# Two late norms' sums of squares on VectorE, and other round sizes in the first ConvGLU

## The chip, the cores and the metric

The kernel runs on one core of a Trainium2 chip. The metric is the device time of one execution in microseconds. A core has five engines with a queue of instructions each: TensorE (PE in the profile, its weight loads PEld), VectorE (DVE), ScalarE (ACT), GpSimd (POOL) and SyncE (SP), which here issues the weight transfers. Each engine works through its queue in order; semaphores make it wait for others. SBUF is the working memory; PSUM, which takes TensorE's results, has eight banks of 512 numbers on each of 128 partitions.

## The reference: what is computed

Two layers over 512 latent tokens and 256 context tokens of width 1024. The first mixes tokens by windowed attention, the second by a bidirectional gated linear recurrence (HGRN2). Each layer ends with a ConvGLU of inner width 2816. Before every mixer and every ConvGLU stands an RMS norm with a scale and a shift. Cut to what matters here:

```python
def rms_norm(x, gain):
    y = x * lax.rsqrt(jnp.mean(x * x, axis=-1, keepdims=True) + EPS)
    return y * gain

def conv_glu(h, w_up, conv_w, conv_b, w_down):
    gate, val = jnp.split(h @ w_up, 2, axis=-1)
    return (jax.nn.silu(dwconv3(gate, conv_w, conv_b)) * val) @ w_down

# each layer
hx = rms_norm(x, norm1_g) * (1 + sc1) + sh1      # and hc from ctx
x  = x + g1 * mixer(hx, hc)                      # and ctx in the first layer
hx2 = rms_norm(x, norm2_g) * (1 + sc2) + sh2
x  = x + g2 * conv_glu(hx2, ...)                 # and ctx in the first layer
```

## The kernel before

**Layout.** The streams lie transposed in SBUF: eight tiles d of 128 features by tokens, `xl` for the 512 latent tokens and `xc` for the 256 context tokens. Every product is done in a split form: each operand is a high part (a ScalarE copy) and a low part (a VectorE subtraction of the high part), and a k tile takes three TensorE products, high by high, high by low and low by high. `load_w` makes such weight operands: one transfer into a raw buffer (two of them, tag `wr`), then per operand the copy at L117 and the subtraction at L118. An operand (`operand`, L84) is a pair of 512-column buffers, taken in turn from several pools; in the first ConvGLU these are one of four pairs and one of two.

**Norms.** A norm needs the sum over all features of x squared, for each token. `square_acc` takes a tile d: ScalarE squares it (L513), into the accumulator `acc` itself for the first tile, else into a buffer `sq` of which there are two; then an addition puts it into `acc` (L515). `row_factor` sums `acc` over the partitions with TensorE (`nss`, L524), takes the power -0.5 on GpSimd (L429), builds a diagonal on VectorE (L529) and spreads it with TensorE (`nR`, L533) into the row factor `R`. The factor is multiplied in after the next product, so that product needs only the scaled but not yet normalized operand that `scaled` makes: a ScalarE copy with a scale (L362) and a VectorE instruction for the low part (L363).

`square_acc` is called in three places. In `attn_out`, the norm ahead of the first ConvGLU, the addition is on VectorE. In `done0`, which the last round of the first ConvGLU calls for each finished tile d, and in `hgrn_out`, ahead of the second ConvGLU, it is on GpSimd.

**The first ConvGLU.** `ffn` (L958) works on 22 column tiles of the inner width. `up(ft)` loads the two weight blocks of a tile, computes gate and value, by seven products of half size (`gate_pair`), the convolution, the SiLU and the product, and leaves the split tile `g` in one of five buffers (pool `gpA`, five, L1345). A round holds some column tiles, as `ROUNDS[0]` says: after its tiles it computes one tile of the next round ahead, and then the down product of its own. The down product takes four passes `dp`; a pass loads the weights of 256 output features for all tiles of the round, as two halves (`cols=True`: an operand holds four k tiles of 128 columns, so a half with more than four takes a second operand), and works on two output tiles d of 128 features. Each d takes two PSUM banks (latent and context) of the eight, and six TensorE products per tile of the round, and ends with two VectorE instructions that add the gated result to `xl` and `xc` (L1023). In the last round nothing is computed ahead; there the first pass does all tiles but the last for both halves before the last one:

```python
part = dp == 0 and not ahead
if part:
    for j in range(2):
        down(j, range(nf - 1))
```

and `done0` runs for tile d after the L1023 of tile d+1: squares and sum, then `scaled` for the recurrence's input `hn2`.

**After it.** `hgrn` takes over the PSUM banks for its own pools and begins with `front(0)`: `pf`, whose weights are loaded like the others, over all eight k tiles of `hn2`. Only after that product comes `row_factor`. At its end `hgrn_out` does the output product `ho`, adds it to `xl` (L895), and scales and squares each tile; the second ConvGLU's first gate product `pd` runs before its `row_factor`.

**Order.** The program order isn't the order on the engines. A planner simulates the timeline while the kernel is built, and puts ready instructions on each engine by priority, which is the program order, save that weight splits are moved ahead (`high_priority(offset=W_AHEAD)`, 180 places). The result is a fixed queue for each engine.

Of the kernel before, what the change touches and what calls it, by code (L numbers as in the profile page):

```python
# [12 lines left out]
ALU = mybir.AluOpType  # L13
# [14 lines left out]
NFF = DFF // P  # L28
EPS = 1e-6
NEG = -1e30  # L30
ROUNDS = ((3, 4, 4, 4, 3, 4), (8, 7, 7))
W_AHEAD = 180
PER_UNIT = 3.2

# [38 lines left out]
class Kernel:  # L73
# [430 lines left out]
    def segs(self, lat_only):  # L504
        return [(0, LAT, self.xl)] + ([] if lat_only else [(LAT, TOK, self.xc)])

    def square_acc(self, d, acc, lat_only, tmp, tag="ny", first=None, eng=None):
        nc = self.nc
        n = LAT if lat_only else TOK
        first = d == 0 if first is None else first  # L510
        sq = acc if first else tmp.tile([P, TOK], F32, tag=tag, name="sq", bufs=2)
        for lo, hi, x in self.segs(lat_only):
            nc.scalar.activation(sq[:, lo:hi], x[:, d], AF.Square)  # L513
        if not first:
            (eng or nc.vector).tensor_tensor(acc[:, :n], acc[:, :n], sq[:, :n], op=ALU.add)  # L515

    def row_factor(self, acc, lat_only, tmp, pp, tag, width, R, sh, dg):

# [439 lines left out]
    def ffn(self, l, hs, R, rows, lat_only, tmp, acp, bk, gp, done, side=None):  # L958
# [14 lines left out]
        def up(ft):  # L973

            ws_ = [self.wcols(wup, ft * P, P), self.wcols(wup, DFF + ft * P, P)]
            ops = self.load_w(ws_) if lat_only else self.load_pair(ws_, tmp)
            if side:
                next(side, None)

            G = tmp.tile([P, 2 * half + 2], F32, tag="G", name="G", bufs=gb)  # L980
            gg = tmp.tile([P, 2 * half], F32, tag="ny", name="gg", bufs=2)
            (self.gate_plain if lat_only else self.gate_pair)(ft, ops, hs, G, gg, R, rows, half, tmp, bank)
            nc.vector.tensor_copy(ap(G[:, 0:1], 0, (TW + 1, nv)), G[:, 1 + SH:1 + SH + nv])
            cb = tmp.tile([P, 2], F32, tag="cb", name="cb")
            nc.vector.tensor_scalar(cb[:, :nv], G[:, 1 + SH:1 + SH + nv], ws[:, ft:ft + 1], cw[:, 66 + ft:67 + ft], op0=ALU.mult, op1=ALU.add)
            u = tmp.tile([P, n], F32, tag="nt", name="u", bufs=gb)
            nc.scalar.activation(u, G[:, 1:1 + n], AF.Copy, scale=cw[:, 22 + ft:23 + ft])
            nc.vector.scalar_tensor_tensor(u, G[:, 0:n], cw[:, ft:ft + 1], u, op0=ALU.mult, op1=ALU.add)
            nc.vector.scalar_tensor_tensor(u, G[:, 2:2 + n], cw[:, 44 + ft:45 + ft], u, op0=ALU.mult, op1=ALU.add)
            for v, c, m in segs:  # L990
                nc.scalar.activation(u[:, c:c + m], u[:, c:c + m], AF.Silu, bias=cb[:, v:v + 1])
                nc.vector.scalar_tensor_tensor(gg[:, c:c + m], gg[:, c:c + m], gg[:, SH + v:SH + v + 1], u[:, c:c + m],
                                               op0=ALU.subtract, op1=ALU.mult)
            g2 = gp.tile([P, 2, n], F32R, tag="g", name="g")
            nc.scalar.activation(g2[:, 0], gg[:, :n], AF.Copy)  # L995
            nc.vector.tensor_tensor(g2[:, 1], gg[:, :n], f(g2[:, 0]), op=ALU.subtract)
            return g2

        f0, late, ahead = 0, None, []
        for r, nf in enumerate(ROUNDS[l]):  # L1000
            gt = ahead + [up(ft) for ft in range(f0 + len(ahead), f0 + nf)]
# [272 lines left out]
    def hgrn_out(self, part, hn, acc, tmp, pj):  # L1274
        nc = self.nc
        self.shifts(1, 1, hn)
        wout = self.a["hgrn_w_out"][0]
        oh = part[0]
        act = lambda k: (oh[:, 0, k], oh[:, 1, k])
        for dp in range(KT // 2):  # L1280
            if dp < 2:
                w, ps, ks = part[1][dp], part[2][dp], (KT - 1,)
            else:
                w = self.load_w([self.wcols(wout, d * P, P) for d in (dp, dp + 4)])
                ps = pj.tile([P, 1024], F32, tag="pj", name="ho")
                ks = range(KT)
            for j in range(2):
                d = dp + 4 * j
                pd = ps[:, 512 * j:512 * j + 512]
                for _ in self.mm_steps(w[j], ks, act, [(pd, 0)], first=dp >= 2):  # L1290
                    pass
                self.add_gated(1, 2, d, pd, True)
            for d in (dp, dp + 4):
                self.scaled(1, 1, d, hn, True)
                self.square_acc(d, acc, True, tmp, "sg", first=(d == 0), eng=nc.gpsimd)


    def dump(self, name, t):
# [3 lines left out]
    def run(self, stop=99):  # L1302
        nc, a = self.nc, self.a
# [26 lines left out]
        tmp = self.pool(es, "tmpA", 1)  # L1330
        acp = self.pool(es, "accA", 1)
        acc = Rp.tile([P, TOK], F32, tag="acc", name="acc0")
# [20 lines left out]
        accs = []  # L1353

        def done0(d, bank):
            if d == 0:
                hn2.append(self.hn_tile(hb, "hn2"))
                accs.append(Rp.tile([P, TOK], F32, tag="acc", name="acc1"))
                self.shifts(1, 0, hn2[0])
            self.square_acc(d, accs[0], False, tmp, eng=nc.gpsimd)  # L1360
            self.scaled(1, 0, d, hn2[0], False)

        self.ap_, self.ap_tag = Rp, "acc"
        self.ffn(0, hs, R, rows, False, tmp, acp, bk, gp, done0, (x for r in (0, 1, 2) for x in self.ada_steps(1, r, bk, "ps", 512)))
        if stop == 3:
            self.dump_x(); rs.close(); es.close(); hss.close(); hB.close(); pjs.close(); top.close(); return
# [15 lines left out]
        acc = Rp.tile([P, LAT], F32, tag="acc", name="acc2")  # L1382
# [10 lines left out]
        tmp = self.pool(es, "tmpB", 2)  # L1393
# [59 lines left out]
```

## Time and profile before

| | us |
|---|---|
| median of 3 runs | 1876.24 |
| lowest and highest run | 1875.39, 1877.27 |
| profiled execution | 1872.88 |
| its span in the profile | 1871.1 |
| TensorE busy | 1801.3 (96%) |
| VectorE busy | 1214.1 (65%) |
| GpSimd busy | 247.4 (13%) |
| mean granted TensorE clock | 0.988 |

Times in the profile count from the start of the span. Busy time is the time in which an engine has an instruction in it. A row of a timeline gives the start, the duration, the engine, the line, the operation, the output and inputs by the program's names, the shapes and a count, where neighbouring instructions of a kind are put together; in brackets stands the idle time of the engine before it, and what ended that. The granted clock is the share of its full rate that TensorE was given.

### The profile page before, as it was taken

Reading aid. Unit: us, or ns where it says so; the run is one execution under the profiler, and the core shown is the slowest. Engines: PE = TensorE matmul, PEld = TensorE weight load, DVE = VectorE, ACT = ScalarE, POOL = GpSimd, SP = SyncE. Lnnn points to the kernel's source line nnn. Section 1 sums busy time; section 2 is a strip of 40 time slices with the busy share of each in tenths; the row PEclk is TensorE's granted clock in tenths of the full one; section 3 lists DMA queues with packets and bytes.
Section 4 is the critical chain, followed back from the end, with each engine's and each line's share of the span. In section 5 each row is a group of like instructions: output and inputs, shape, how many; then the busy total and the mean of one; then the engine's idle time right before and its main releaser. Section 6 shows DMA issues by size and latency. Waiting matters only on the chain.

```text
span 1871.1 us, 32302 instructions
## 1 busy us (share of the span) xinstructions
PE 1801.3 (96%) x13326; PEld 1576.9 (84%) x13326; DVE 1214.1 (65%) x2243; ACT 754.7 (40%) x1478; POOL 247.4 (13%) x233
## 2 busy tenths in 40 slices
PE   6999999998999999999998999999998999999998
PEld 4976786787888888989887888988886799899997
DVE  5575667466867686766777676777676655455462
ACT  4354555465534252434354333333332443233332
POOL 1233333103201000101013101111110200000000
PEclk9999999998999999999998999999999999999999
DMA  9204104232333333233313212122220332333321
GB/s 309 66 23 158 47 24 169 68 102 68 124 113 102 113 124 113 91 113 124 113 61 90 58 35 58 35 57 58 57 69 24 90 91 91 90 96 96 92 82 65
DMA packets 204416, 166.44 MB, mean 89 GB/s; under 512 B 5149, under 2 KB 198254, under 8 KB 199150
## 3 DMA queue, kind: packets, MB, share of 16 engines
q1 hardware_dynamic: 196608, 160.47, 27.8%
q10 hardware_dynamic: 7662, 3.92, 0.7%
q8 instruction: 105, 1.72, 0.4%
q14 instruction: 41, 0.34, 0.1%
HBM read 162.27 MB, written 2.10 MB: 88 GB/s over the span
## 4 chain that ended last, share of the span: by engine, by line
PE 87%; DVE 5%; DMA 4%; issue 2%; ACT 1%; POOL 1%; SPq 0%; ACTq 0%; POOLq 0%; DVEq 0%
PE dn L170 15%; PE pd L170 13%; PE pZ L188 8%; PE pf L170 8%; PE pV L188 4%; PE pjq L598 4%; PE pv L170 4%; PE ao L170 4%; PE ho L170 3%; PE pq L170 3%; PE pv L824 2%; PE pt L816 2%; PE ada L309 2%; PE pY L188 2%; PE pgate L170 2%; PE kv L598 2%
## 5 line engine op out<-in xcount | busy, mean ns | idle before, releaser
L117 ACT ACTIVATE wh<-wr 128x512 fp32r<-128x512 f32 (+1 forms) x320 | 193.0, 618 | 452.3 <-DMA wr<-in_ffn_w_up 74.8
L118 DVE TENSOR_TENSOR wl<-wr,wh 128x512 fp32r<-128x512 f32 (+1 forms) x320 | 223.6, 705 | 140.3 <-ACT wh L117 138.3
L170 PE MATMUL dn<-g,wh 128*128 128x512 f32 (+1 forms) x1056 | 263.3, 357 | 2.2 <-ACT g L995 2.2
L170 PE MATMUL pd<-hn,wh 128*128 128x256 f32 (+1 forms) x1408 | 227.3, 284 | 0.9 <-issue 0.9
L170 PEld LDWEIGHTS dn<-g,wh 128*128 128x128 f32 x1056 | 175.4, 189 | 32.7 <-ACT g L995 2.8
L170 PEld LDWEIGHTS pd<-hn,wh 128*128 128x128 f32 x1408 | 194.2, 190 | 2.5 <-issue 2.3
L188 PE MATMUL pZ<-hs,wh 128*128 128x386 f32 x704 | 185.2, 345 | 3.0 <-ACT wh L140 1.5
L170 PE MATMUL dn<-g,wl 128*128 128x512 f32 (+1 forms) x528 | 159.4, 356 | 0.0
L140 ACT ACTIVATE wh<-wr 128x512 fp32r<-128x512 f32 x132 | 81.6, 628 | 167.9 <-DMA wr<-in_ffn_w_up 47.4
L170 PE MATMUL pd<-hn,wl 128*128 128x256 f32 x704 | 141.8, 283 | 0.0
L188 PEld LDWEIGHTS pZ<-hs,wh 128*128 128x128 f32 x704 | 128.0, 190 | 15.7 <-ACT wh L140 4.4
L141 DVE TENSOR_TENSOR wl<-wr,wh 128x512 fp32r<-128x512 f32 x132 | 94.0, 717 | 53.6 <-ACT wh L140 53.5
L170 PE MATMUL pf<-hn,wh 128*128 128x512 f32 (+1 forms) x512 | 119.3, 349 | 9.7 <-DVE xc L1023 8.8
L188 PE MATMUL pZ<-hs,wl 128*128 128x386 f32 x352 | 119.4, 343 | 2.2 <-DVE wl L141 2.2
L926 POOL TENSOR_TENSOR gg<-gg,R 128x772 f32<-128x772 f32 x22 | 53.9, 2449 | 458.3 <-DVE gg L925 446.6
L170 PEld LDWEIGHTS pd<-hn,wl 128*128 128x128 f32 x704 | 109.0, 190 | 0.0
L1023 DVE SCALAR_TENSOR_TENSOR xl<-dn,mod,xl 128x512 f32<-128x512 f32 x72 | 53.9, 748 | 73.7 <-PE dn L170 73.6
L170 PEld LDWEIGHTS dn<-g,wl 128*128 128x128 f32 x528 | 87.4, 188 | 14.8
L170 PEld LDWEIGHTS pf<-hn,wh 128*128 128x128 f32 x512 | 80.9, 192 | 22.5 <-ACT wh L117 9.1
L188 PE MATMUL pV<-hs,wh 128*128 128x386 f32 x352 | 92.2, 341 | 5.0 <-ACT hs L392 5.0
L598 PE MATMUL pjq<-wh,hn 128*128 128x256 f32 x384 | 77.8, 291 | 0.0
L188 PEld LDWEIGHTS pZ<-hs,wl 128*128 128x128 f32 x352 | 66.7, 190 | 6.6 <-DVE gg L925 3.4
(299 smaller groups left out, 3807.1 us busy)
## 6 DMA issues: line engine op xcount, KB each, us to landing
wr<-in_ffn_w_up SPq DMA_DIRECT2D x88, 512.0 KB, 5.1
wada<-in_ada_w SPq DMA_DIRECT2D x40, 1024.0 KB, 4.8
wr<-in_hgrn_w_in SPq DMA_DIRECT2D x40, 512.0 KB, 4.2
ar<-in_ada_w SPq DMA_DIRECT2D x32, 256.0 KB, 7.1
wr<-in_ffn_w_down SPq DMA_DIRECT2D x16, 512.0 KB, 4.1
wr<-in_ffn_w_down SPq DMA_DIRECT2D x8, 896.0 KB, 4.7
wr<-in_attn_w_in SPq DMA_DIRECT2D x6, 1024.0 KB, 8.1
wr<-in_attn_w_out SPq DMA_DIRECT2D x8, 512.0 KB, 4.9
```

The source lines that it names most:

```text
L117: nc.scalar.activation(wh, src, AF.Copy)
L118: nc.vector.tensor_tensor(wl, src, f(wh), op=ALU.subtract)
L140: nc.scalar.activation(ops[i][0], src, AF.Copy)
L141: nc.vector.tensor_tensor(ops[i][1], src, f(ops[i][0]), op=ALU.subtract)
L170: nc.tensor.matmul(o, lhsT=wt, rhs=at[:, t0:t0 + o.shape[1]], start=(first and n == 0 and i == 0), stop=(last and n == len(ks) - 1 and i = ...
L188: self.nc.tensor.matmul(ps, lhsT=wt, rhs=at, start=(first and k == 0 and i == 0), stop=(k == nk - 1 and i == 2), skip_group_check=not first)
L309: nc.tensor.matmul(ps[32 * j:32 * j + 32, 0:512], lhsT=self.cs[:, k, :], rhs=raw[:, j * 512:(j + 1) * 512], start=(k == 0), stop=(k == KT ...
L598: nc.tensor.matmul(out, lhsT=x, rhs=y[:, wk], start=(start and k == 0 and j == 0), stop=(stop and k == KT - 1 and j == 2))
L816: nc.tensor.transpose(pt[:, j * P:(j + 1) * P], pr[j][:, b * P:(b + 1) * P], self.ident)
L824: nc.tensor.matmul(pv[a * HD:(a + 1) * HD, 0:256], lhsT=V[:, tl, g, :], rhs=pT[:, a * 256:(a + 1) * 256], start=(b == 0), stop=(b == len(t ...
L926: times = lambda eng, o, x, y: eng.tensor_tensor(o, x, y, op=ALU.mult)
L1023: nc.vector.scalar_tensor_tensor(x[:, d], o, self.modc(l, v, 5, d), x[:, d], op0=ALU.mult, op1=ALU.add)
```

## The change

Three lines. The additions of the sums of squares in `done0` and in `hgrn_out` go from GpSimd to VectorE, seven in each place, of 768 and of 512 columns. The first ConvGLU's six rounds hold 3, 3, 4, 4, 3 and 5 column tiles, where they held 3, 4, 4, 4, 3 and 4. The second ConvGLU's rounds stay.

```diff
-ROUNDS = ((3, 4, 4, 4, 3, 4), (8, 7, 7))
+ROUNDS = ((3, 3, 4, 4, 3, 5), (8, 7, 7))
...
-    def square_acc(self, d, acc, lat_only, tmp, tag="ny", first=None, eng=None):
+    def square_acc(self, d, acc, lat_only, tmp, tag="ny", first=None):
...
         if not first:
-            (eng or nc.vector).tensor_tensor(acc[:, :n], acc[:, :n], sq[:, :n], op=ALU.add)
+            nc.vector.tensor_tensor(acc[:, :n], acc[:, :n], sq[:, :n], op=ALU.add)
...
-                self.square_acc(d, acc, True, tmp, "sg", first=(d == 0), eng=nc.gpsimd)
+                self.square_acc(d, acc, True, tmp, "sg", first=(d == 0))
...
-            self.square_acc(d, accs[0], False, tmp, eng=nc.gpsimd)
+            self.square_acc(d, accs[0], False, tmp)
```

## The prediction, made before the run

> **What bounds the kernel now.** I read the busy shares first, then the busy time by stretches, then the idle spots of TensorE one by one.
>
> ```profile
> span 1871.1 us, 32302 instructions
> PE 1801.3 (96%) x13326; PEld 1576.9 (84%) x13326; DVE 1214.1 (65%) x2243; ACT 754.7 (40%) x1478; POOL 247.4 (13%) x233
> ```
>
> TensorE is busy 96% of the span, and the change removes none of its matrix products. Only its idle time, some 70 us, can be won. The next view gives busy time per stretch (length, then TensorE, weight loads, VectorE, ScalarE, GpSimd, granted clock). The first row is the first ConvGLU up to its end, the second all that TensorE does after the last g tile is ready, the third the stretch up to the recurrence's first product.
>
> ```profile
> 456.00:971.80 515.80, 510.30 (x2898) 460.48 (x2896) 369.11 (x625) 207.73 (x363) 53.87 (x22) 1.00 0.35 109
> 973.55:995.00 21.45, 21.34 (x120) 18.52 (x120) 20.08 (x25) 14.06 (x29) 7.83 (x4) 1.00 0.35 99
> 975.88:1003.62 27.74, 19.05 (x109) 16.47 (x107) 27.74 (x37) 18.02 (x38) 11.28 (x6) 0.91 0.34 95
> ```
>
> TensorE loses 5.5 us in the first 516 us. In the third row VectorE is busy for all 27.74 us, so there the bound has moved to it. TensorE's own rows (start, duration, work, idle before in brackets):
>
> ```profile
> 973.59 2.03 PE L170 MATMUL dn<-g,wh 128*128 128x512 f32 x10 [1.72 <-ACT g L995]
> 994.41 0.52 PE L170 MATMUL dn<-g,wl 128*128 128x512 f32 x2
> 1003.76 1.62 PE L170 MATMUL pf<-hn,wh 128*128 128x512 f32 x4 [8.84 <-DVE xc L1023]
> 1009.26 0.88 PE L170 MATMUL pf<-hn,wh 128*128 128x512 f32 x4
> 1010.32 0.86 PE L170 MATMUL pf<-hn,wh 128*128 128x512 f32 x4
> ```
>
> Two idle spots belong to the changed stage: 1.72 us for the last g, and 8.84 us from the last down product (994.93) to pf, which waits for the last L1023, because its banks are the old dn banks. A third loss follows: pf needs 5.5 us for its first three k (1003.76 to 1009.26) where one k at full rate takes 1.06 us (1009.26 to 1010.32), so 5.5 - 3.2 = 2.3 us. The granted clock (the number after GpSimd) says why:
>
> ```profile
> 972.00:974.00 2.00, 0.41 (x2) 0.37 (x3) 1.03 (x3) 0.84 (x1) 0.00 (x0) 1.00 0.00 0
> 1006.00:1008.00 2.00, 2.00 (x8) 1.72 (x7) 2.00 (x2) 0.09 (x1) 2.00 (x1) 0.50 0.00 0
> 1010.00:1012.00 2.00, 2.00 (x14) 1.74 (x13) 0.00 (x0) 0.00 (x0) 0.00 (x0) 1.00 0.24 74
> ```
>
> After the gap of 8.84 us the clock is at half, and back by 1010; after the one of 1.72 us it is whole. Why VectorE is late, its rows show beside those of GpSimd:
>
> ```profile
> 980.70 0.74 DVE L363 SCALAR_TENSOR_TENSOR hn<-xl,gs,hn 128x512 fp32r<-128x512 f32 x1
> 981.35 2.08 DVE L363 SCALAR_TENSOR_TENSOR hn<-xc,gs,hn 128x256 fp32r<-128x256 f32 x1
> 983.36 2.34 DVE L118 TENSOR_TENSOR wl<-wr,wh 128x512 fp32r<-128x512 f32 x1
> 985.62 2.38 DVE L363 SCALAR_TENSOR_TENSOR hn<-xl,gs,hn 128x512 fp32r<-128x512 f32 x1
> 987.93 0.74 DVE L1023 SCALAR_TENSOR_TENSOR xl<-dn,mod,xl 128x512 f32<-128x512 f32 x1
> 988.59 0.47 DVE L363 SCALAR_TENSOR_TENSOR hn<-xc,gs,hn 128x256 fp32r<-128x256 f32 x1
> 988.98 0.47 DVE L1023 SCALAR_TENSOR_TENSOR xc<-dn,mod,xc 128x256 f32<-128x256 f32 x1
> 990.43 2.36 DVE L363 SCALAR_TENSOR_TENSOR hn<-xl,gs,hn 128x512 fp32r<-128x512 f32 x1
> 992.72 0.48 DVE L363 SCALAR_TENSOR_TENSOR hn<-xc,gs,hn 128x256 fp32r<-128x256 f32 x1
> 996.63 2.02 DVE L363 SCALAR_TENSOR_TENSOR hn<-xc,gs,hn 128x256 fp32r<-128x256 f32 x1
> 998.57 1.28 DVE L118 TENSOR_TENSOR wl<-wr,wh 128x512 fp32r<-128x512 f32 x2
> 1003.14 0.47 DVE L1023 SCALAR_TENSOR_TENSOR xc<-dn,mod,xc 128x256 f32<-128x256 f32 x1
> ```
>
> ```profile
> 980.94 4.21 POOL L515 TENSOR_TENSOR acc<-acc,sq 128x768 f32<-128x768 f32 x2 [18.24 <-ACT sq L513]
> 985.61 1.85 POOL L515 TENSOR_TENSOR acc<-acc,sq 128x768 f32<-128x768 f32 x1 [0.46 <-ACT sq L513]
> 990.39 1.85 POOL L515 TENSOR_TENSOR acc<-acc,sq 128x768 f32<-128x768 f32 x1 [2.94 <-ACT sq L513]
> 996.24 2.13 POOL L515 TENSOR_TENSOR acc<-acc,sq 128x768 f32<-128x768 f32 x1 [4.00 <-ACT sq L513]
> 1002.30 1.94 POOL L515 TENSOR_TENSOR acc<-acc,sq 128x768 f32<-128x768 f32 x1 [3.93 <-ACT sq L513]
> ```
>
> Each VectorE row above 2 us starts during a GpSimd add and ends 0.3 to 0.6 us after it. L1023, which has one operand in PSUM, keeps its 0.47 us even in the add of 1002.30. So an instruction with both operands in SBUF stands still during an add.
>
> **The sums of squares.** From start to start the five slowed instructions take 2.01, 2.26, 2.31, 2.29 and 1.94 us. The same forms undisturbed take 0.39 (988.59 to 988.98), 0.60 (half of the 1.28 row's pair, 998.57 to 999.77), 0.66, 0.66 and 0.39. Removed: 8.1 us. Added are the adds themselves, which the earlier norm already does on VectorE:
>
> ```profile
> L515 POOL TENSOR_TENSOR acc<-acc,sq x14: 1286/1748/2257, 980.9 to 1482.3; 128x768 f32<-128x768 f32 x7, 128x512 f32<-128x512 f32 x7
> L515 DVE TENSOR_TENSOR acc<-acc,sq x7: 950/959/960, 377.6 to 430.2; 128x768 f32<-128x768 f32 x7
> ```
>
> At 0.96 us, about 0.9 from start to start, and with five of seven ahead of the last L1023 (tiles 1 to 5), that is 4.5 us. A new wait comes with them: an add stands in VectorE's queue until ScalarE has squared its tile, with L363 and the next L1023 behind it. L363 of that tile needs a ScalarE copy made beside those squares, and VectorE is behind ScalarE here, so I cost that wait at nothing (up to a square, 0.6 us, where VectorE has caught up). Net 3.6 us off VectorE's queue. Its 27.7 us hold 27.7 - 8.1 = 19.6 us of other work.
>
> [...]
>
> **The rounds.** The last round does 240 products instead of 192 (4 passes x 2 halves x 5 tiles x 6). Two passes fit the eight banks, so before the last g it can do 2 x 2 x 4 x 6 = 96 instead of 72, and after it 144 instead of the 120 of the second stretch. At 21.34/120 = 0.178 us that is 25.6 us. The work in all being the same, TensorE ends where it did, less the saved idle time: 24 products more are 4.3 us of cover for the 1.72 us wait. I take 1.4 saved (0 to 1.7): end at 993.5, last g at 967.9.
>
> VectorE after that: 2.3 us until the first sum is done (973.59 to 975.88), 19.6, 4.5, and the split fifth tile: its weight operand holds 512 columns, so each half of a pass adds a copy pair of 128 columns, six of them late. The width's price comes from
>
> ```profile
> L118 DVE TENSOR_TENSOR wl<-wr,wh 128x512 fp32r<-128x512 f32 x30 | 21.4, 723 | 12.9 <-ACT wh L117 12.9
> L118 DVE TENSOR_TENSOR wl<-wr,wh 128x384 fp32r<-128x384 f32 x16 | 8.7, 553 | 3.9 <-ACT wh L117 3.9
> wr<-in_ffn_w_down SPq DMA_DIRECT2D x8, 896.0 KB, 4.7
> ```
>
> that is 0.55 - 2 x 0.17 = 0.2 to 0.3 us; six at 0.3 make 1.8. Sum 28.2, so VectorE is done at 996.1 and pf starts at 996.2, a gap of 2.7 us. If the six recurrence copies in the queue (3.6 us) slip behind, TensorE bounds, and the gap is one pair of L1023, 0.66 + 0.47, and 0.15 of signalling: 1.3. I take 2.0: pf at 995.5, **8.3 us earlier**.
>
> Of the clock loss of 2.3 us I keep 1.2 (0 to 2.3), as 2.0 us lies between a gap with a drop and one without. [...]
>
> What costs nothing: the down weights are the same bytes in the same number of transfers on SP's queue; the 640 KB of a 5-tile pass land in less than the 4.7 us of the 896 KB row, within a pass of 60 x 0.178 = 10.7 us. The earlier rounds end at other tiles; their last chains lie under the tile computed ahead. I bound this by -1 to +2, for the 5.5 us of idle time in 516, and take 0. After pf starts, two adds (1.8 us) precede the eighth k tile, needed 7.4 us later.
>
> The second norm (hgrn_out) I cost at 0:
>
> ```profile
> 1450.00:1484.00 34.00, 31.71 (x133) 24.60 (x134) 25.46 (x34) 17.64 (x31) 10.38 (x7) 0.91 0.37 104
> 1474.23 0.71 PE L170 MATMUL ho<-oh,wh 128*128 128x512 f32 x2 [1.36 <-ACT hn L362]
> 1482.29 1.29 POOL L515 TENSOR_TENSOR acc<-acc,sq 128x512 f32<-128x512 f32 x1 [4.09 <-ACT sq L513]
> 1486.77 0.95 PE L524 MATMUL nss<-cst,acc 128*128 128x2 f32 x8
> 1490.12 1.19 PE L533 MATMUL nR<-dg,cst 128*128 128x512 f32 x1 [2.41 <-DVE dg L529]
> ```
>
> Here VectorE is busy 25.5 of 34 us and TensorE 31.7, so VectorE isn't the bound; seven adds of 512 columns at 0.6 to 0.7 us take the place of 10.4 us of GpSimd. The last add ends 3.2 us before TensorE gets to nss, behind the first gate product, which hides it. The wait of 2.41 us comes after the sums. Bounds: +0.7 if that cover went, -1.4 if a less disturbed VectorE also ends the wait of 1.36 us.
>
> Sum: -8.3 - 1.1 = **-9.4 us**. The profiled execution took 1872.88 us (span 1871.1 and 1.8 around it), so 1863.5; the median of the runs stands 3.36 above it: 1866.8.
>
> **The rivals.** *Half of it* (0.17): the order on each engine is planned ahead. If the last L1023 is put behind tile 6's add and two L363 (0.9 + 1.06), pf starts at 998.2, the clock drop stays, and the 1.72 wait may too: 4 us won, 1872. For it: in the rows of before L1023 does stand behind L363. Against: dn comes earlier in the program.
>
> *Squares without a slot* (0.10), the slower one. The squares have two buffers, freed by the add. On a saturated VectorE it comes late, and ScalarE waits before its third square; if it has the weight copies (L117) of the last passes behind that, TensorE stalls. Four tiles come within 4.3 us and give VectorE 4 x (1.1 + 1.06) + 3 x 0.9 = 11 us of work, so each of two passes could wait 7 us: 994.8 + 14 = 1008.8, 5 us late, 1881. It decides above 9 us of stall. Against it: copies are issued with a lead of 180 places.
>
> *The stretching isn't GpSimd's* (0.05): then VectorE keeps the 8.1 us and ends at 1004.2, 0.5 later than now: 1876.7. The undisturbed L1023 speaks against it.
>
> *A new stall elsewhere* (0.13): earlier boundaries, two 3-tile rounds on end, another plan. One of 5 to 9 us there eats most: 1871 to 1876, beyond 13 us slower. The 5.5 us in 516 speak against much.
>
> **How the numbers follow.** The forecast has 0.55, with 1862 to 1870 of its own. Below, the low end has both bounds at their best (gap 1.3, no clock loss, 1.72 gone, 1.4 at the second norm): 14 us, 1862. The high end takes in half of it, no relief and most of the new stalls: 1877. A measurement here tells about 0.2%, 3.75 us, from no change. Faster by more: 0.55, half of *half of it*, 0.04 of the stalls, 0.67 in all. Within: 0.09 + 0.05 + 0.07 = 0.21. Slower: 0.12.
>
> **What would show it.** Right: no VectorE row of L363 or L118 above 1.5 us in the tail; 14 more VectorE adds; pf's idle time 1.3 to 2.8 us; the last g's wait below 0.5; about 144 products after it. Wrong: idle time over 4 us before pf, TensorE waiting on ScalarE copies in the last round, or idle time before the last g well above 5.5 us.

## The result, and the profile after

The changed kernel takes 1864.1 us (median of six runs, 1862.16 to 1865.07) beside 1876.74 us for the kernel before on the same chip (1875.39 to 1879.46): a ratio of 0.9932, 95% interval 0.9922 to 0.9942. The forecast was 1866.8 us. The profiled execution took 1863.46 us, 9.42 less than that of before, where 9.4 was forecast. That the sum came out so near is partly luck, as the sections below show.

From the page of the changed kernel, its span and the engines' busy times:

```profile
span 1861.4 us, 32314 instructions
PE 1798.5 (97%) x13326; PEld 1575.2 (85%) x13326; DVE 1214.4 (65%) x2265; ACT 755.0 (41%) x1486; POOL 218.8 (12%) x219
```

GpSimd has 14 instructions and 28.6 us less, VectorE 22 more (14 adds, and eight L118 for the split fifth tile), in the same busy time: the adds took the place of the stretching.

The changed kernel's timeline of TensorE at the end of the first ConvGLU: the first product on the last g, the last down products, and `pf`.

```profile
967.13 1.62 PE L170 MATMUL dn<-g,wh 128*128 128x512 f32 x6
...
992.46 0.52 PE L170 MATMUL dn<-g,wl 128*128 128x512 f32 x2
994.91 0.97 PE L170 MATMUL pf<-hn,wh 128*128 128x512 f32 x4 [1.94 <-DVE xc L1023]
```

The wait before the last g is gone, and the 8.84 us before `pf` have become 1.94. The same stretches as before, by busy time (columns as in the prediction): up to the last g, from there to the last down product, and the start of `pf`.

```profile
455.40:967.13 511.73, 504.24 (x2873) 456.47 (x2872) 372.99 (x629) 207.48 (x365) 48.93 (x22) 1.00 0.35 108
967.13:992.98 25.85, 25.82 (x144) 22.14 (x144) 24.44 (x45) 19.23 (x43) 0.00 (x0) 1.00 0.38 108
...
996.00:998.00 2.00, 2.00 (x13) 1.77 (x12) 2.00 (x4) 2.00 (x5) 0.00 (x0) 1.00 0.00 0
...
```

Behind the last g stand 144 products in 25.85 us, TensorE busy all the time, and after the gap the clock stays whole. But in the first row TensorE is idle for 511.73 - 504.24 = 7.5 us, where it was 5.5. VectorE's groups in the tail show no stretched instruction any more; first the changed kernel from 966 us on (count, busy time, mean ns of one, idle time before), then the kernel before from 973 us on:

```profile
L118 DVE TENSOR_TENSOR wl<-wr,wh 128x512 fp32r<-128x512 f32 x11 | 7.3, 690 | 4.1 <-ACT wh L117 4.1
L515 DVE TENSOR_TENSOR acc<-acc,sq 128x768 f32<-128x768 f32 x7 | 6.7, 957 | 0.0
L363 DVE SCALAR_TENSOR_TENSOR hn<-xl,gs,hn 128x512 fp32r<-128x512 f32 x8 | 6.0, 751 | 0.5 <-ACT hn L362 0.5
...
L363 DVE SCALAR_TENSOR_TENSOR hn<-xc,gs,hn 128x256 fp32r<-128x256 f32 x8 | 3.9, 484 | 0.0
...
L118 DVE TENSOR_TENSOR wl<-wr,wh 128x128 fp32r<-128x128 f32 x6 | 1.7, 285 | 0.0
```

```profile
L363 DVE SCALAR_TENSOR_TENSOR hn<-xl,gs,hn 128x512 fp32r<-128x512 f32 x7 | 9.0, 1280 | 0.0
L118 DVE TENSOR_TENSOR wl<-wr,wh 128x512 fp32r<-128x512 f32 x10 | 8.2, 846 | 0.0
L363 DVE SCALAR_TENSOR_TENSOR hn<-xc,gs,hn 128x256 fp32r<-128x256 f32 x7 | 6.5, 924 | 0.0
```

**Where the time went, stage by stage.** Each column is a difference of two starts in TensorE's timeline of the one profiled execution (or an end and a start): S, the start of the first `pV`; A, from there to the end of the last `dn`; B, the gap before `pf`; C, from `pf` to the norm's sum `nss`; D, from there to the start of the last row of `U` products of the recurrence (L1197); F, to the second ConvGLU's first `pd`; G, from there to the end of the span. The experiments' rows are used below.

| | S | A | B | C | D | F | G | span |
|---|---|---|---|---|---|---|---|---|
| before | 443.3 | 551.6 | 8.8 | 10.8 | 421.0 | 45.4 | 390.1 | 1871.1 |
| changed | 442.7 | 550.2 | 1.9 | 8.6 | 423.2 | 44.9 | 389.9 | 1861.4 |
| e0_before_again | 441.8 | 554.5 | 7.8 | 10.4 | 421.6 | 45.4 | 391.2 | 1872.7 |
| e1_squares_only | 444.5 | 553.5 | 3.4 | 10.8 | 420.1 | 44.9 | 390.0 | 1867.2 |
| e2_rounds_only | 444.1 | 551.2 | 7.6 | 10.2 | 422.9 | 45.4 | 390.1 | 1871.4 |
| e3_first_norm | 441.6 | 550.3 | 1.9 | 8.6 | 423.0 | 45.4 | 389.8 | 1860.6 |
| e5_gp_adds | 444.5 | 552.9 | 6.8 | 11.2 | 421.1 | 44.7 | 389.8 | 1871.1 |
| e6_gp_memset | 442.9 | 550.5 | 1.6 | 8.6 | 421.4 | 44.8 | 390.0 | 1859.7 |
| e7_344335 | 442.9 | 552.6 | 1.9 | 8.6 | 421.6 | 44.6 | 390.0 | 1862.1 |
| e8_sum_early | 441.1 | 551.5 | 1.9 | 8.6 | 421.1 | 44.8 | 387.1 | 1856.0 |
| e9_sum_earlier | 443.7 | 550.8 | 1.9 | 10.1 | 421.2 | 44.7 | 387.1 | 1859.5 |
| e10_after_again | 442.9 | 550.3 | 1.9 | 8.6 | 423.1 | 44.8 | 389.9 | 1861.4 |

Before to changed: S -0.6, A -1.4, B -6.9, C -2.2, D +2.2, F -0.5, G -0.2, in all -9.6 of the 9.7 us (the rest is rounding). S lies ahead of everything that any of these kernels changes and still spreads over 3.4 us, so one profile's span alone tells little below that; the stages are what is compared.

### The profile page after: what moved, and what is told of

Its sections match the earlier page's. It is cut to its first block, busy times and chain, and to the rows that moved or that the text cites. A ratio compares the mean times of both kernels' runs of the same rounds, so it can differ in the third digit from the quotient of the medians.

```text
span 1861.4 us, 32314 instructions
## 1 busy us (share of the span) xinstructions
PE 1798.5 (97%) x13326; PEld 1575.2 (85%) x13326; DVE 1214.4 (65%) x2265; ACT 755.0 (41%) x1486; POOL 218.8 (12%) x219
## 4 chain that ended last, share of the span: by engine, by line
PE 88%; DMA 4%; DVE 4%; ACT 1%; issue 1%; POOL 0%; SPq 0%; ACTq 0%; POOLq 0%; DVEq 0%
PE dn L170 15%; PE pd L170 14%; PE pZ L188 8%; PE pf L170 8%; PE pV L188 4%; PE pjq L598 4%; PE pv L170 4%; PE ao L170 4%; PE ho L170 3%; PE pq L170 3%; PE pv L824 3%; PE pt L816 2%; PE ada L309 2%; PE pgate L170 2%; PE kv L598 2%; DMA wr<-in_ffn_w_up 2%
## 5 line engine op out<-in xcount | busy, mean ns | idle before, releaser
L117 ACT ACTIVATE wh<-wr 128x512 fp32r<-128x512 f32 (+2 forms) x328 | 194.5, 608 | 462.4 <-DMA wr<-in_ffn_w_up 76.9
L118 DVE TENSOR_TENSOR wl<-wr,wh 128x512 fp32r<-128x512 f32 (+2 forms) x328 | 220.0, 678 | 137.6 <-ACT wh L117 137.0
L141 DVE TENSOR_TENSOR wl<-wr,wh 128x512 fp32r<-128x512 f32 x132 | 95.9, 733 | 47.9 <-ACT wh L140 46.6
L926 POOL TENSOR_TENSOR gg<-gg,R 128x772 f32<-128x772 f32 x22 | 48.9, 2224 | 456.5 <-DVE gg L925 443.6
L1023 DVE SCALAR_TENSOR_TENSOR xl<-dn,mod,xl 128x512 f32<-128x512 f32 x72 | 53.9, 749 | 73.7 <-PE dn L170 73.7
```

The costliest lines, as they stand in the source:

```text
L117: nc.scalar.activation(wh, src, AF.Copy)
L118: nc.vector.tensor_tensor(wl, src, f(wh), op=ALU.subtract)
L141: nc.vector.tensor_tensor(ops[i][1], src, f(ops[i][0]), op=ALU.subtract)
L926: times = lambda eng, o, x, y: eng.tensor_tensor(o, x, y, op=ALU.mult)
L1023: nc.vector.scalar_tensor_tensor(x[:, d], o, self.modc(l, v, 5, d), x[:, d], op0=ALU.mult, op1=ALU.add)
```

## The experiments

Every time below is a median with its runs' range, every ratio is to runs of the kernel before on the same chip beside it. The edits are shown against the changed kernel.

### The two parts apart: e0, e1, e2, e3

*e0_before_again* is the kernel before, unaltered.

> The kernel before once more, unchanged, to see how its profiled execution stands to its runs: its first profile took 1872.88 us where its runs took 1875.4 to 1879.5. If the first profile was a lucky one, this span lies 2 to 5 us above 1871.1, and the difference lies in single stretches (for one the last head of the recurrence, 1388 to 1440, where the wait for the hgrn_w_out transfer stands), not in the changed stage: idle time before pf 8.8 us again, within 0.3. If the two kernels differ by 12 us in every pair of executions, the span is 1871 again and the runs stay 3 us above it for a reason outside the profile.

1875.38 us (1873.78 to 1879.35), ratio 0.9997 (0.9987 to 1.0008). Stage A is 2.9 us longer than in the first profile of the same kernel. Its rows, the wait for the last g and the clock (the number before the last two) behind it:

```profile
973.47 3.00 PE L170 MATMUL dn<-g,wh 128*128 128x512 f32 x10 [2.01 <-ACT g L995]
```

```profile
975.00:977.00 2.00, 2.00 (x8) 1.71 (x8) 0.06 (x1) 0.00 (x0) 0.00 (x0) 0.50 0.00 0
977.00:979.00 2.00, 2.00 (x12) 1.74 (x12) 2.00 (x4) 1.17 (x3) 0.00 (x0) 0.85 0.00 0
```

Here the wait is 2.01 us, not 1.72, and TensorE works at half rate for some 3 us after it. The profile on which the prediction rests was a lucky execution of the kernel before: there the clock stayed whole behind the wait (1.00).

*e1_squares_only* leaves the rounds as they were.

```diff
-ROUNDS = ((3, 3, 4, 4, 3, 5), (8, 7, 7))
+ROUNDS = ((3, 4, 4, 4, 3, 4), (8, 7, 7))
```

> Both sums of squares on VectorE, the rounds as before (3, 4, 4, 4, 3, 4). My theory (VectorE bounds the stretch after the last g, and GpSimd's adds hold it up by 8.1 us): after the last g at 973.5 VectorE needs 2.3 + 19.6 + 4.5 = 26.4 us, so pf starts at 1000.1 instead of 1003.8, with 5 us of idle time before it and the clock drop kept: 3.7 us faster than before, ratio 0.998. Rival (the rounds make all of it, an add costs VectorE what it frees): within 1 us of before, idle time before pf still 8 to 9 us. Second rival (the adds alone were the trouble): 9 us faster, as the whole change.

1867.45 us (1866.26 to 1870.43), ratio 0.9954 (0.9940 to 0.9968): 8.8 us faster than before, well over twice what was expected. TensorE's waits in its tail, and the clock behind the second:

```profile
975.25 3.44 PE L170 MATMUL dn<-g,wh 128*128 128x512 f32 x10 [2.25 <-ACT g L995]
...
1001.38 0.95 PE L170 MATMUL pf<-hn,wh 128*128 128x512 f32 x4 [3.37 <-DVE xc L1023]
```

```profile
1002.00:1004.00 2.00, 2.00 (x9) 1.66 (x9) 2.00 (x4) 0.98 (x3) 0.00 (x0) 0.58 0.00 0
```

The gap is 3.37 us where about 5 was expected, so the squares alone take 5.5 of its 8.84 us; the clock still drops (C 10.8). In its profile the last g's wait is 2.25 us with a clock drop too, which costs A 1.9 us beside the first profile of before. By medians the gain is larger than by profiles (8.8 against 3.9 in the span, where S alone takes back 1.2): the profiled execution of e1 lies 1.5 us above its median, the first one of the kernel before 3.4 us below. What the other executions did isn't seen.

*e2_rounds_only* has the new rounds and the adds on GpSimd in both places.

```diff
-            nc.vector.tensor_tensor(acc[:, :n], acc[:, :n], sq[:, :n], op=ALU.add)
+            (eng or nc.vector).tensor_tensor(acc[:, :n], acc[:, :n], sq[:, :n], op=ALU.add)
```

with `eng=nc.gpsimd` in `done0` and in `hgrn_out`, as before.

> The rounds 3, 3, 4, 4, 3, 5, the sums of squares on GpSimd as before. My theory: the last g comes at 967, and VectorE then needs 2.3 + 19.6 + 8.1 + 1.8 = 31.8 us, so pf starts at about 999, idle time before it 6 us, clock drop kept; the wait of 1.72 us before the last g is gone. 4 to 5 us faster than before, ratio 0.9975, and the rows of L363 and L118 above 2 us are still there. Rival (the rounds make all of it): 9 to 10 us faster, idle time before pf about 2 us. Second rival (the adds alone were the trouble): within 1 us of before.

1873.02 us (1868.82 to 1877.08), ratio 0.9984 (0.9972 to 0.9995): 3.2 us faster. The last g's wait is gone; the stretching stays, and so does most of the gap, 7.59 us where 6 was expected. TensorE's row and a group of VectorE's:

```profile
1002.88 1.65 PE L170 MATMUL pf<-hn,wh 128*128 128x512 f32 x4 [7.59 <-DVE xc L1023]
```

```profile
L363 DVE SCALAR_TENSOR_TENSOR hn<-xc,gs,hn 128x256 fp32r<-128x256 f32 x8 | 10.0, 1253 | 0.0
```

*e3_first_norm* is the changed kernel, but with `hgrn_out`'s adds on GpSimd again (`eng=nc.gpsimd` there alone).

> The new rounds and the first norm's adds (done0) on VectorE, but hgrn_out's adds on GpSimd as before. My theory: the second norm is worth nothing (-1.4 to +0.7 us), so this equals the whole change within 1 us, ratio to before about 0.9935 to 0.995. Rival: the second norm's adds carry part of the 12.6 us by which the medians differ (the profiled executions differ by 9.4): then this run is 1.5 us or more slower than the whole change, with more idle time between 1441 and 1482 of the changed kernel's time.

1863.32 us (1862.65 to 1868.28), ratio 0.9937 (0.9921 to 0.9952), the changed kernel's time within the interval. The second norm decides nothing that the times can tell. The stages do tell a little: F is 45.4 us in all four kernels with those adds on GpSimd and 44.6 to 44.9 in all eight with them on VectorE, half a microsecond.

So the gain is the first norm's squares, with the rounds behind them: 8.8 and 3.2 us alone, 12.6 together. In B and C together they help each other: 19.6 us before, 14.2 with the squares, 17.8 with the rounds, 10.5 with both, that is 5.4 and 1.8 apart but 9.1 together. Only both bring the gap below 2 us (1.94 in the changed kernel), and the clock is whole behind it (1.00).

### Is it GpSimd's reading of SBUF? e5, e6

Both are the changed kernel with work on GpSimd that nobody waits for, in `done0`. *e5_gp_adds* reads SBUF:

```diff
+            if d:
+                scr = tmp.tile([P, TW], F32, tag="nt", name="scr")
+                nc.gpsimd.tensor_tensor(scr[:, :LAT], self.xl[:, d], self.xl[:, d], op=ALU.add)
+                nc.gpsimd.tensor_tensor(scr[:, LAT:TOK], self.xc[:, d], self.xc[:, d], op=ALU.add)
             self.square_acc(d, accs[0], False, tmp)
```

> The changed kernel, with VectorE's own sums of squares, and beside them two additions on GpSimd for each column tile from the second on in the late norm of the first ConvGLU: x + x of the 512 latent columns and of the 256 context columns, into scratch that nobody reads. [...] Theory (GpSimd's adds stretch VectorE's two-input instructions, and that is what the old squares cost): the rows of L363, L118 and L515 in the last round go back from 0.5 to 1.3 us to about 2 us where an addition overlaps them, VectorE's queue grows by about 1.2 us for each of seven tiles, and TensorE's idle time before the first product of the hgrn goes from 1.94 us to 8 to 11 us; the kernel is 6 to 11 us slower than the changed kernel, about 1870 to 1875 us. Rival (the old form was slow because VectorE and the squares waited for GpSimd's results in turn, not because of a shared path): VectorE's rows stay as they are in the changed kernel, the idle time stays within 0.5 us of 1.94 us, and the time is that of the changed kernel within 1.5 us, 1863 to 1866 us.

1869.87 us (1867.59 to 1873.56), ratio 0.9974 (0.9965 to 0.9983), 5.6 us slower than e6 beside it. The profiled execution, 1873.56 us, is the slowest of its ten, so its span overstates what the adds cost. VectorE's and GpSimd's groups from 966 to 1006 us, and TensorE's row:

```profile
L118 DVE TENSOR_TENSOR wl<-wr,wh 128x512 fp32r<-128x512 f32 x10 | 8.6, 883 | 1.7 <-ACT wh L117 1.7
L363 DVE SCALAR_TENSOR_TENSOR hn<-xl,gs,hn 128x512 fp32r<-128x512 f32 x7 | 6.6, 938 | 0.0
L1023 DVE SCALAR_TENSOR_TENSOR xl<-dn,mod,xl 128x512 f32<-128x512 f32 x8 | 5.9, 741 | 0.9 <-PE dn L170 0.9
...
L118 DVE TENSOR_TENSOR wl<-wr,wh 128x128 fp32r<-128x128 f32 x6 | 3.2, 525 | 0.0
```

```profile
L1363 POOL TENSOR_TENSOR scr<-xl 128x512 f32<-128x512 f32 x7 | 7.6, 1086 | 32.6 <-DVE xl L1023 16.9 <-ACT hn L362 15.7
L1364 POOL TENSOR_TENSOR scr<-xc 128x256 f32<-128x256 f32 x7 | 6.1, 871 | 0.0
```

```profile
1004.23 1.65 PE L170 MATMUL pf<-hn,wh 128*128 128x512 f32 x4 [6.79 <-DVE xc L1023]
```

*e6_gp_memset* only writes: a copy of two columns on VectorE sets the moment, then GpSimd fills the scratch twice (`scrs[0]` is one such tile).

```diff
+                c = 752 + 2 * d
+                nc.vector.tensor_copy(scrs[0][:, c:c + 2], self.xl[:, d, 0:2])
+                for _ in range(2):
+                    nc.gpsimd.memset(scrs[0][:, 0:c + 2], 0.0)
```

> The changed kernel, and for each column tile from the second on in the late norm of the first ConvGLU one copy of two columns on VectorE (which only fixes the moment) and behind it two fills of 768 columns of scratch with zeros on GpSimd, which write SBUF and read nothing from it. Theory that any GpSimd access stretches VectorE: the rows of L363, L118 and L515 in the last round are stretched as they were under GpSimd's additions, and the idle time before the first product of the hgrn goes from 1.94 us to 6 us or more. Rival, that only reads collide: those rows stay at their 0.48 to 1.28 us, the idle time grows only by the seven small copies, 0.5 to 1 us, to about 2.5 to 3 us, and the kernel is within 2 us of the changed one's 1864 us. [...]

1864.27 us (1862.35 to 1864.88), ratio 0.9938 (0.9924 to 0.9951), the changed kernel's time. The same views:

```profile
L118 DVE TENSOR_TENSOR wl<-wr,wh 128x512 fp32r<-128x512 f32 x11 | 7.4, 686 | 3.4 <-ACT wh L117 3.4
...
L363 DVE SCALAR_TENSOR_TENSOR hn<-xl,gs,hn 128x512 fp32r<-128x512 f32 x8 | 6.0, 746 | 0.4 <-ACT hn L362 0.4
...
L118 DVE TENSOR_TENSOR wl<-wr,wh 128x128 fp32r<-128x128 f32 x6 | 1.7, 283 | 0.0
```

```profile
L1368 POOL MEMSET scr<- 128x768 f32 x2 | 1.5, 742 | 2.8 <-DVE scr L1366 2.7
```

```profile
995.00 0.97 PE L170 MATMUL pf<-hn,wh 128*128 128x512 f32 x4 [1.59 <-DVE xc L1023]
```

GpSimd is busy in both, for 13.7 us and for seven pairs of fills of about 1.5 us (10.3 us). Under the adds VectorE's instructions with two SBUF operands are stretched (L118 883 ns against 686 under the fills, L363 938 against 746), and L1023, which has one in PSUM, keeps its 741 ns (749 in the changed kernel); under the fills nothing is stretched (690 and 751 in the changed kernel). The first rival is out: no result of GpSimd is waited for in e5, and the stretching came back. So is the theory that any access of GpSimd does it. In these two runs the stretching came with the adds, which read SBUF, and not with the fills, which only write it.

The size is smaller than expected. Between these two kernels the stretching of the three groups shown, taken as the difference of means times e5's count, is 2.0 + 1.3 + 1.5 = 4.8 us; L363's 256 columns (643 against 480 ns, seven times) and L515 (1030 against 953 ns, five times) make it 6.3. The gap grows by 5.2. In the kernel before 8.1 us were lost, all in five instructions, for about as much work on GpSimd. An add that meets L1023 costs nothing, by its rows (741 ns); that the rest of the difference lies in what each add happens to meet is a guess, which no run shows.

### Does the order of the other rounds matter? e7

```diff
-ROUNDS = ((3, 3, 4, 4, 3, 5), (8, 7, 7))
+ROUNDS = ((3, 4, 4, 3, 3, 5), (8, 7, 7))
```

> The changed kernel with the first ConvGLU's rounds at 3, 4, 4, 3, 3, 5 column tiles instead of 3, 3, 4, 4, 3, 5: the fifth and the last round are the same, the second and fourth have changed places. Theory (only the length of the last round matters, since it puts 144 instead of 96 products behind the last tile that VectorE makes): the same as the changed kernel within 1.5 us, no idle time before the last tile's products and 1.9 to 2.1 us before the first product of the hgrn. Rival (where the short rounds stand matters too, since each round's end has products that wait for a late tile): the first ConvGLU's product time of 550.3 us moves by 2 us or more in one direction or the other, with waits on ScalarE's copies of a tile inside an earlier round.

1865.88 us (1864.16 to 1867.6), ratio 0.9947 (0.9935 to 0.9960), 1.6 us above e6 beside it with overlapping ranges. The tail is the same (B 1.9, no wait for the last g). Stage A is 2.4 us longer than the changed kernel's, and one row and the clock behind it carry most of that:

```profile
675.64 0.44 PE L188 MATMUL pZ<-hs,wl 128*128 128x386 f32 x1 [2.25 <-DVE wl L141]
```

```profile
676.00:680.00 4.00, 4.00 (x16) 4.00 (x15) 3.13 (x5) 1.95 (x4) 0.00 (x0) 0.57 0.64 201
```

At a clock of 0.57, 4 us hold 1.7 us less work. The other part is a group that the prediction did not have: the products of the second layer's modulation (`ada`), which the first ConvGLU takes in between its tiles. Over stage A they are, in this kernel and in the changed one:

```profile
L309 PE MATMUL ada<-wada,cs 128*32 128x512 f32 x184 | 26.6, 605 | 0.4 <-DMA wada<-in_ada_w 0.4
```

```profile
L309 PE MATMUL ada<-wada,cs 128*32 128x512 f32 x184 | 25.5, 605 | 0.5 <-DMA wada<-in_ada_w 0.5
```

The same 184 products hold TensorE 1.1 us less with 3, 3, 4, 4, 3, 5, and that in all eight profiles with these rounds (25.5 or 25.6), with 26.6 us in all four with others (before, e0, e1, e7). So the order of the middle rounds does matter in these profiles, by about 1 us of TensorE's time, and by a wait of 2.25 us behind which the clock dropped (0.57); the time itself doesn't separate the two at this accuracy. Why the products overlap better there wasn't tried.

### A further step: e8, e9, e10

In the changed kernel TensorE waits again at the second ConvGLU's norm. *e8_sum_early* moves the norm's sum into the first gate product (`gate_plain`):

```diff
-            for _ in self.mm_steps(ops[j], range(KT), act, [(o, lo) for o, (lo, _) in zip(ps, cols)]):
-                pass
+            for n, _ in enumerate(self.mm_steps(ops[j], range(KT), act, [(o, lo) for o, (lo, _) in zip(ps, cols)])):
+                if n == 3:
+                    next(rows, None)
```

> The changed kernel, with one step moved in the second ConvGLU: the four summing products of its norm and the factor from them are issued after the fourth step inside the first gate product, instead of behind that product. In the changed kernel TensorE is idle 1.92 us before that product and then 2.46 us before the norm's spreading products (which wait for VectorE's diagonal), and its clock falls behind the second of these. Theory that this second wait is only a matter of where the sum stands: the 2.46 us go, and with them about 1 us of lower clock; 2 to 4 us faster than the changed kernel, 1860 to 1862 us. Rival (VectorE is busy with the last scaled tiles, so the sum waits for its last square and holds the queue there): the wait moves ahead to the summing products, up to 2 us, and the time stays within 1 us of the changed kernel.

1861.79 us (1858.96 to 1863.41), ratio 0.9929 (0.9916 to 0.9943). The changed kernel's row and clock at the spreading products, then those of e8:

```profile
1480.73 1.59 PE L533 MATMUL nR<-dg,cst 128*128 128x512 f32 x2 [2.46 <-DVE dg L529]
```

```profile
1480.00:1484.00 4.00, 3.27 (x11) 2.52 (x12) 1.56 (x5) 0.81 (x2) 0.00 (x0) 0.65 0.00 0
```

```profile
1476.92 1.10 PE L533 MATMUL nR<-dg,cst 128*128 128x512 f32 x2 [1.14 <-DVE dg L529]
```

```profile
1480.00:1484.00 4.00, 4.00 (x36) 4.00 (x35) 2.43 (x4) 3.29 (x5) 0.00 (x0) 1.00 0.02 4
```

The wait is 1.3 us shorter and the clock stays whole: G falls from 389.9 to 387.1 us. The theory holds for that much; 1.14 us of the wait are left.

*e9_sum_earlier* puts `n == 1` in place of `n == 3`.

> As the kernel with the norm's sum after the fourth step of the second ConvGLU's first gate product, but after its second step. There the summing products began at 1473.52 us though VectorE's last square was added by 1470.94 us, and TensorE still waited 1.14 us for the diagonal before the spreading products. Theory (the sum stood later than its data needed): begun 2.3 us earlier, at about 2.3 us after the first gate product's start, the sum doesn't wait, and the 1.14 us wait before the spreading products goes; about 1 us faster than that kernel and 3.5 to 4.5 us faster than the changed one run beside it, and the stretch from the first gate product to the end of the span, 389.9 us in the changed kernel and 387.1 us there, becomes about 386 us. Rival: the sum now waits for VectorE's last square on TensorE's queue, and the stretch stays at 387 us or above.

*e10_after_again* is the changed kernel, unaltered, beside it.

> The changed kernel once more, unaltered, as the measure for the kernel beside it and for what changes from one profiled execution to the next. Theory (the slower clock of about 8 us that the first profile of the changed kernel shows in the last head's output products is chance, as it stood in three of the six kernels that share those instructions and in none of the other three): time within 0.15% of the first, 1862 to 1867 us; the stretch from the norm's sum to the last U products is either 421.0 to 421.8 us with the clock at 1.00 throughout or 422.9 to 423.3 us with the clock down to about 0.8. Rival (the change itself costs those 2.1 us): 423 us again, with the same lower clock.

e9 took 1861.77 us (1861.47 to 1862.77), ratio 0.9928 (0.9916 to 0.9940); e10 1864.05 us (1863.33 to 1867.56), ratio 0.9944 (0.9932 to 0.9956). The ranges don't overlap: 2.3 us faster than the changed kernel, and this version, about 0.7% below the kernel before, is the best of the study. But e9 isn't a new step. Its instructions stand in the same order as e8's on every engine: the planner, which places ready instructions by its own timeline, had put the sum 4.6 us after the gate product's start in both. So e9 is e8 once more, the last microsecond was not reached, and whether it can be is open.

e10 settles one thing about stage D. Both profiles of the changed kernel and that of e3 show 423.0 to 423.2 us, and the kernels e8 and e9, whose instructions stand in the same order up to the end of D, 421.1 and 421.2. The clock's own times say why. In the first profiles of both kernels every change of the granted clock inside the span lies a whole number of steps of 3.413 us from every other; in that of the changed kernel, for example, the clock is at half from 1402.69 to 1406.10, from 1436.82 to 1447.06 and from 1481.19 to 1484.61. These are 1, 3 and 1 steps, 10 and 13 apart from start to start. So in these profiles the clock changed only on a grid of 3.41 us, and where a wait falls on that grid differs from one execution to the next. The wait in the last head, first in e10, then in e8, each with the stretch of the grid that holds its end and the next one:

```profile
1401.55 0.46 PE L1132 MATMUL lv<-Q,Y 128*32 128x32 f32 x32 [1.65 <-ACT v L1103]
...
1399.43:1402.85 3.42, 1.62 (x45) 1.22 (x38) 3.42 (x7) 2.66 (x5) 0.00 (x0) 1.00 0.03 5
1402.85:1406.26 3.41, 3.41 (x10) 2.66 (x9) 3.41 (x7) 0.72 (x2) 0.00 (x0) 0.50 0.00 0
```

```profile
1400.57 0.46 PE L1133 MATMUL lv<-Q,Y 128*32 128x32 f32 x32 [1.65 <-DVE Q L1157]
...
1399.15:1402.57 3.42, 1.86 (x38) 1.58 (x39) 3.42 (x7) 2.19 (x4) 0.00 (x0) 1.00 0.02 5
1402.57:1405.98 3.41, 3.41 (x17) 2.74 (x16) 3.41 (x7) 1.36 (x3) 0.00 (x0) 1.00 0.00 0
```

The wait is 1.65 us in both. In e10 all of it falls into one stretch, of which TensorE is busy for 1.62 us, and the clock is at half through the next: half of 3.41 us, 1.7 of the 2.1 us. In e8 it begins at 1398.92, before the stretch; TensorE is busy for 1.86 us there, and the clock stays whole. (An earlier wait, 1.00 us in e10 and 0.41 in e8, ends before either stretch begins.) The expectation's "three of six" counted e2, whose 422.9 us has another cause: its clock is whole there. Nothing in the program differs between e10 and e8 up to this point, so the 2.1 us aren't a price of the change; that they stood in both profiles of the changed kernel is chance, as far as these rows tell.

## Why the prediction was right, point by point

**The sums of squares: right.** No row of L363 or L118 above 1.49 us is left in the tail, where the longest holds three copies, no single instruction above 0.76, and the adds cost 957 ns each, as taken (0.96). e5 and e6 show the cause. *The stretching isn't GpSimd's* is out.

**The gap before `pf`: right, its size with some luck.** 2.0 us taken, 1.94 measured; the split fifth tile's six copies 1.7 us, 1.8 taken. The 2.0 was chosen between two workings, 2.7 with VectorE's whole queue ahead of the last L1023 and 1.3 with TensorE alone. The trace has the second one with one L363 in the way: TensorE ends at 992.98, an L363 runs from 993.05, the last two L1023 follow from 993.72, and the next copy (L118) stands behind them, at 994.77. It took both parts, which the working had added up in one queue: by e1 alone 3.37, by e2 alone 7.59.

**The wait for the last g: right as a wait, wrong as a gain.** 1.4 of 1.72 us were taken as won, all of it went, and stage A is 1.4 us shorter. But the step on the earlier rounds, taken at 0, was mis-sized: TensorE's idle time before the last g grew from 5.5 to 7.5 us, the upper end of what was allowed. TensorE's waits by group over the stage show the trade, first before, then changed (idle time last):

```profile
L170 PE MATMUL dn<-g,wh 128*128 128x512 f32 x352 | 131.4, 397 | 2.2 <-ACT g L995 2.2
L188 PE MATMUL pZ<-hs,wl 128*128 128x386 f32 x336 | 113.6, 342 | 2.2 <-DVE wl L141 2.2
```

```profile
L170 PE MATMUL dn<-g,wh 128*128 128x512 f32 x352 | 130.7, 396 | 0.0
L188 PE MATMUL pZ<-hs,wl 128*128 128x386 f32 x336 | 113.6, 341 | 4.4 <-DVE wl L141 4.4
```

What was won at the last g was lost again to waits for split weights (L141) in the earlier rounds. They don't stand at the rounds' ends, where the prediction looked for them: the three longest (1.30, 1.53 and 1.22 us, at 631.95, 732.91 and 834.65) lie inside the gate and value products, some 25 us behind the end of a down product. That A still fell is for the most part the 1.1 us of the `ada` products, which the prediction did not have. What the removed wait is worth beyond that is the clock: in e0 and e1 it was 2.01 and 2.25 us and the clock dropped behind it (to 0.50 in e0), in the first profile of before 1.72 and it didn't (1.00).

**The clock behind the gap: mis-sized.** A loss of 1.2 us of 2.3 was kept; none was left (C 8.6 against 10.8). The bound of no loss came nearer in this profile. In e9, behind nearly the same gap (1.90 us), 1.5 us were lost.

**The second norm: 0 taken, half a microsecond won,** in F, inside the bounds.

**Not foreseen: D.** 2.2 us more, for the most part by the clock in the last head, which e10 and e8 show to be chance; with it the profile's sum met the forecast, as the unkept clock loss (1.1), F and S (0.5 and 0.6) went the other way.

**The median: mis-sized.** I added 3.36 us to the profiled time because the first runs of before stood that far above their profile. That offset belonged to one execution and not to the kernel: the median of e0 stands 0.6 us above its profile, and so does the changed kernel's. These 2.7 us are the whole error of the forecast. *Half of it*, *squares without a slot* and *a new stall elsewhere* did not come: `pf` starts at 994.91 and not at 998.2, TensorE is busy for 25.82 of 25.85 us behind the last g, and the added idle time stayed at 2 us. In the range, the terms named for the low end add up to 13 us and not to 14; the other 1 is the lower bound on the earlier rounds.

## What to carry to other kernels

Here GpSimd, off the critical path, slowed VectorE, which was on it, by 8.1 us in five instructions: look in the groups of VectorE's rows for the same form with two durations, and see what GpSimd reads at that time; moving the work to VectorE cost 6.7 us of adds and still won (the gap 8.84 to 3.37 us in e1). A larger last round, or any work that needs nothing late, is the cover for a chain that must end on another engine; but ask which wait in the other rounds takes the place of the one removed. And before adding an offset from profile to median, profile the kernel before a second time: one wait near 2 us made a stage of the same kernel 2.9 us longer here.

## What was not expected of the hardware

The clock dropped after much shorter waits than the 8.84 us behind which the first profile had shown it at half. Single waits of TensorE after which the granted clock was whole: 1.56 and 1.72 us (the kernel before, at 676.00 and 973.59), 1.53 and 1.92 us (the changed kernel, at 732.91 and 1471.52), and 1.59 to 1.94 us before `pf` in six kernels. After these it fell to about a half: 2.01 (e0), 2.25 (in e1 and e7), 2.46 (the changed kernel) and 3.37 us (e1), and also 1.65 us in e10's last head and 1.90 us in e9. The last, TensorE's row in e9 and two stretches of the grid on which the clock changes (e10); then the same two stretches in e8, where the wait is 1.91 us:

```profile
996.39 0.97 PE L170 MATMUL pf<-hn,wh 128*128 128x512 f32 x4 [1.90 <-DVE xc L1024]
...
994.04:997.46 3.42, 1.52 (x9) 1.06 (x9) 3.42 (x7) 1.43 (x4) 0.00 (x0) 1.00 0.53 153
997.46:1000.87 3.41, 3.41 (x13) 2.94 (x12) 3.41 (x6) 1.82 (x4) 0.00 (x0) 0.50 0.00 0
```

```profile
992.96:996.38 3.42, 1.88 (x11) 1.65 (x12) 3.42 (x7) 1.43 (x4) 0.00 (x0) 1.00 0.42 127
996.38:999.79 3.41, 3.41 (x22) 2.98 (x21) 3.06 (x5) 1.10 (x3) 0.00 (x0) 1.00 0.00 0
```

The waits are alike to 0.01 us. In e9 the whole of it lies in one stretch and TensorE is busy for 1.52 us of it; in e8 it begins in the stretch before, which leaves 1.88 us busy, and the clock stays whole. In these two rows, as in those of the last head, what differs is how much of the wait falls into one stretch. Other full stretches of the grid lie close together: the clock stayed whole behind 1.69 us busy (the kernel before, 971.20 to 974.61) and 1.60 (the changed kernel, 993.09 to 996.51), and fell behind 1.61 (the changed kernel, 1399.28 to 1402.69). In a stretch with small products it fell behind more: 2.04 us busy in the kernel before (100.80 to 104.21), and 0.50 in the next one; what counts there isn't shown. So of the waits between 1.65 and 1.94 us here some were followed by half the clock and some were not, behind those listed from 2.01 to 3.37 us it fell each time, and a fall cost 1.5 us in e9 (its C of 10.1 beside the changed kernel's 8.6) and 2.6 in e5 (11.2, behind a gap of 6.79 us).
